# The scan of an RWKV-7 and Hyena block: ScalarE and VectorE in program order, the preparation in 35 pieces, weight splits one batch ahead

## The chip, the cores and the metric

The kernel runs on one core of a Trainium2 chip. The metric is device time in microseconds (us). A profiled execution gives the trace: the busy times of TensorE (PE, with PEld for its weight loads), VectorE (DVE), ScalarE (ACT) and GpSimd (POOL), the DMA queues (SyncE, SP, issues most of them), and the clock that TensorE was granted.

## The reference

Two layers on 256 latent tokens and 256 context tokens of width 2048. Layer 0 mixes tokens with RWKV-7: a recurrence over time in both directions, first over the context and then, from its final state, over the latents. Layer 1 mixes with Hyena (gated long convolutions by FFT). Each is followed by a squared-ReLU MLP, and everything is modulated by vectors computed from `c` (adaLN). The part that the change touches is the recurrence:

```python
def step(S, inp):
    w_t, k_t, v_t, kk_t, b_t = inp[:5]
    S = (S * w_t[:, :, None, :]
         - jnp.einsum('bhvk,bhk->bhv', S, kk_t)[..., None] * b_t[:, :, None, :]
         + v_t[..., None] * k_t[:, :, None, :])
    out = jnp.einsum('bhvk,bhk->bhv', S, inp[5]) if emit else None
    return S, out
```

`S` is 64 x 64 for each of 32 heads; `v = xv @ w_v` and the readout's `r = xr @ w_r` are projections of the mixed tokens.

## The kernel before

The scan is done in chunks of 64 tokens, so that it becomes matrix products. Four heads make a group (`g`, 0 to 7); a group has 8 steps (`i`), four over the context and four over the latents, and each step handles one chunk forward and one backward. `rwkv_scan` (line 780) loops over groups and steps, and cuts each step into three slots (`j` = 0, 1, 2; `n = 3 * i + j` counts the 24 slots of a group).

The chain that runs from step to step is `scan_step` (line 1086), one piece a slot. Slot 0: PE multiplies the chunk's values `VU` and the state `Z` into `pr`, ACT copies it to `rhs` (line 1112). Slot 1: PE applies the inverted triangular matrix `Y`, and ACT writes the result into `VU` (lines 1130 and 1131). Slot 2: PE makes the new state, ACT copies it to `Z` (line 1142). On PE other work stands between these:

- `scan_products` (line 985): the next step's matrices, masked and copied out of PSUM to `NT` by DVE and `KR` by ACT and DVE. Its diagonal matrices (line 993) come from DVE.
- `scan_prepare` (line 1020): the whole preparation of group g + 1, a generator that is advanced by `SCHED[n]` pieces a slot. `scan_prep` makes the operands of four units (two streams, two pairs of heads) from loads of `kx`, `rb`, `cum`, `a` and, for the latents, `rx`. `scan_m` makes the matrices `Mn` to invert. Then 31 rounds of two DVE instructions each (lines 1047 and 1049) invert 32 x 32 blocks; two DVE transposes (lines 1054 and 1055) and ACT's copies with masks (lines 1059 and 1060) write them into `Y`; the products `G` and `py` join the blocks.
- `scan_readout`: norm, bonus and gate of group g - 1, one piece a step at slot 2.
- `ada_scan`: adaLN products, one unit a step.
- `fill_v` and `fill_r` (lines 729 and 747): the projections `v` of group g + 1 and `r` of group g + 2, six pieces a step in slots 1 and 2. Their weights are loaded by SP (`fr`, line 712) and split into two parts by ACT (`fh`, line 133) and DVE (`flo`, line 134); their tokens `fx` are loaded by POOL.

In the last group the Hyena filters take the place of the fills.

What sets the order: a planner simulates the program at compile time and orders each engine's instructions and each DMA queue by priority and simulated readiness. Within the scan PE alone is bound to the program's order: `product` (line 71) ties each product to the one before it by an edge that is only used in planning (`pinned`). The pieces of the chain run at priority `PRI`, the next step's products at `PRJ`. ACT, DVE, SP and POOL are ordered by the planner. At run time each engine executes its instructions in the order it was given. Three PSUM buffers `sg` serve products, preparation and readout in turn.

The functions of the kernel that the change touches, with the line numbers of the profile:

Of the kernel before, what the change touches and what calls it, by code (L numbers as in the profile page):

```python
# [18 lines left out]
P = 128  # L19
# [22 lines left out]

class Kern:
    def __init__(self, nc, tc, I, out, scr, upto=99):
        self.nc, self.tc, self.I, self.out, self.scr = nc, tc, I, out, scr
        self.bg, self.credit, self.rate = [], 0.0, 0.0
        self.upto = upto
        self.wraw, self.wsp = [], []
# [21 lines left out]

    def product(self, out, lhsT, rhs, **kw):

        r = self.nc.tensor.matmul(out, lhsT=lhsT, rhs=rhs, **kw)  # L73
        if self.pinned:
            if self.pinned is not True:
                self.tc.add_manual_dep(r.ins, self.pinned.name, mybir.DependencyInfo(mybir.DependencyClass.NoSync, mybir.DependencyReason.DATA),
                                       reason="order of the scan")
            self.pinned = r.ins
        return r

    pinned = None
# [646 lines left out]

    def fill_v(self, g):

        nc = self.nc
        ps = [self.fl.tile([P, 2, 256], F32, name="fl") for _ in range(2)]
        for k in range(KT):
            if k % 2 == 0:
                w = self.fill_w(self.I["w_v"][0], k, g)
            x = self.fill_x(self.scr["xv"][k])
            for tt in range(4):
                s = slice(tt * P, (tt + 1) * P)
                self.fill_mm(ps[tt // 2][:, tt % 2], (x[:, 0, s], x[:, 1, s]), [a[:, k % 2] for a in w], k, tt % 2)
                if tt % 2:  # L740
                    yield
        for j in range(2):
            t = self.fw.tile([P, 2, 256], F32, name="fe", bufs=2)
            nc.scalar.copy(t, ps[j])
            nc.sync.dma_start(self.scr["v"][g, j * 256 : (j + 1) * 256, :].rearrange("(a p) n -> p a n", p=P), t)

    def fill_r(self, g):
        nc = self.nc
        ps = self.fl.tile([P, 2, 256], F32, name="fl")
        for k in range(0, KT, 2):  # L750
            w = self.fill_w(self.I["w_r"][0], k, g)
            x = self.fill_x(self.scr["xr"][k // 2])
            for q in range(2):
                for i in range(2):
                    self.fill_mm(ps[:, i], [a[:, q, i * P : (i + 1) * P] for a in w],
                                 [x[:, j, q * L : q * L + L] for j in range(2)], k + q, i)
                yield
        t = self.fw.tile([P, 2, 256], F32, name="fe", bufs=2)
        nc.scalar.copy(t, ps)
        nc.sync.dma_start(self.scr["r"][g * 256 : (g + 1) * 256, :].rearrange("(a p) n -> p a n", p=P), t)  # L760

# [7 lines left out]
    def rwkv_begin(self):  # L769

        self.bg = [self.urgent(self.scan_prepare(0), self.PRB)]
        n = 80 - self.NLOW
        for _ in self.beside(self.fill_r(0), 16, itertools.islice(self.low, n // 8), n // 8 + .1):
            self.tick(6.0 / (16 + n // 8))
        for _ in self.beside(itertools.chain(self.fill_v(0), self.fill_r(1)), 48, self.low, n - n // 8 + .1):
            self.tick(self.BEG)
        self.drain()


    def rwkv_scan(self, es, prep_pools, ngroups=KT // 2):  # L780
# [17 lines left out]
        self.pinned = True  # L798
        for g in range(ngroups):

            last = g + 1 == ngroups
            prep = iter(()) if last else self.scan_prepare(g + 1)
            read = self.scan_readout(g - 1) if g else iter(())
            take = lambda it, n: [None for _ in itertools.islice(it, n)]
            if not last:
                fill = itertools.chain(self.fill_v(g + 1), self.fill_r(g + 2) if g + 2 < ngroups else ())
            else:
                prep_pools.close()
# [3 lines left out]
            for i in range(8):  # L812
                nxt = self.scan_products(g, i + 1) if i < 7 else () if last else self.scan_products(g + 1, 0)
                step = self.scan_step(g, i)
                for j in range(3):
                    with self.tc.high_priority(self.PRI):
                        next(step)
                    if j == 0:
                        with self.tc.high_priority(self.PRJ):
                            for _ in nxt:  # L820
                                pass
                    take(prep, self.SCHED[3 * i + j])
                    if j == 1:
                        take(ada, 1)
                    if j == 2:
                        take(read, 1)
                    if last:
                        pin, self.pinned = self.pinned, None
                        with self.tc.issue_after(pin):
                            take(fill, self.NFILT)  # L830
                        self.pinned = pin
                    elif j:
                        take(fill, 3)
                if i == 5 and last:
                    pin, self.pinned = self.pinned, None
                    take(late, 1)
                    self.pinned = pin
            take(prep, 99), take(read, 99), take(fill, 99)
            self.grp.pop(g - 1, None)
        self.pinned = None  # L840
# [3 lines left out]


    SCHED = (2, 1, 2, 1, 2, 1, 0, 2, 2, 1, 2, 2, 2, 2, 2, 2, 2, 2, 1, 1, 1, 0, 2, 2)
# [4 lines left out]
    def scan_open(self, es, prep_pools):  # L851

        self.loaded, self.unit = [], 0
# [46 lines left out]

    def scan_prep(self, g, pi, st, eend, res):
# [7 lines left out]
        if st == 1:  # L909
            rx = ld.tile([P, L], F32, name="rx")  # L910
            nc.sync.dma_start(rx, scr["r"][m * P : (m + 1) * P, :])
        yield
# [3 lines left out]
        eexc = ex[:, 0:524].rearrange("p (d x) -> p d x", d=2)[:, :, 0:260].rearrange("p d (c t) -> p d c t", t=65)[:, :, :, 0:64]  # L916
        nc.scalar.activation(einc, c4(cum), AF.Exp, scale=-EH)
        nc.scalar.copy(eend[:, st, pi, 0, :], ex[:, 64:260:65])
        nc.scalar.copy(eend[:, st, pi, 1, :], ex[:, 261:521:65])
        ei = tp.tile([P, 2, L], F32, name="ei")  # L920
        nc.scalar.activation(ei, cum, AF.Exp, scale=EH)
        bc = lambda a: a[:].unsqueeze(1).broadcast_to([P, 2, L])
        bc4 = lambda a: a[:].rearrange("p (c t) -> p c t", t=64).unsqueeze(1).broadcast_to([P, 2, 4, 64])
        nc.vector.scalar_tensor_tensor(kk, kx, self.col("k_k", m), kk, op0=ALU.mult, op1=ALU.mult)

        KB = self.kbp[g % 2].tile([P, 2, 2, 4, 64], F32, name="KB", bufs=4)
        nc.vector.tensor_tensor(KB[:, 1], c4(a), c4(ei), op=ALU.mult)
        nc.vector.tensor_tensor(KB[:, 1], KB[:, 1], bc4(kk), op=ALU.mult)

        nc.vector.tensor_tensor(self.ard_view(g, pi, 4 * st), bc4(kk), eexc, op=ALU.mult)  # L930
        res["KB", pi, st] = KB
        yield

        kd = KB[:, 0]
        nc.scalar.activation(kd, c4(a), AF.Identity, scale=self.hka[:, 0, m : m + 1], bias=self.hka[:, 1, m : m + 1])
        nc.vector.tensor_tensor(kd, kd, bc4(kx), op=ALU.mult)
        if st == 1:
            nc.vector.tensor_tensor(self.ard_view(g, pi, 3), bc4(rx), einc, op=ALU.mult)
# [3 lines left out]
            nc.vector.tensor_tensor(q4, kd[:, 0], kd[:, 1], op=ALU.add)  # L942
            nc.vector.scalar_tensor_tensor(q, rx, self.col("r_k", m), q, op0=ALU.mult, op1=ALU.mult)
            res["q", pi] = q
        nc.vector.tensor_tensor(kd, kd, c4(ei), op=ALU.mult)
# [39 lines left out]
    def scan_products(self, g, i):  # L985
# [4 lines left out]
        if il == 0:  # L990
            for pi in range(2):
                D_ = self.ard_view(g, pi, 1 + st).rearrange("p d c t -> p (d c) t")
                nc.vector.tensor_tensor(D_, self.id2[:].unsqueeze(1).broadcast_to([P, 8, 64]),
                                        eend[:, st, pi].rearrange("p d c -> p (d c)").unsqueeze(2).broadcast_to([P, 8, 64]), op=ALU.mult)
# [25 lines left out]
    def scan_prepare(self, g):  # L1020
# [21 lines left out]
        nc.gpsimd.memset(fl(W)[:, 0:1024:33], 1.0)  # L1042
        tmp = gp.tile([P, 256], F32, name="tmp", bufs=1)
# [10 lines left out]
        nc.vector.transpose(V[1][:].rearrange("p b t -> p t b"), W[:])  # L1054
        nc.vector.transpose(V[0][:].rearrange("p b t -> p t b"), W[:].rearrange("p i j -> p j i"))

        for d in range(2):
            src = V[d][:, 16 * d : 16 * d + 16, :]
            nc.scalar.activation(Y[:, d, :, 0:32], src, AF.Identity, scale=self.masks[:, 0, 1, 31:32])
            nc.scalar.activation(Y[:, d, :, 32:64], src, AF.Identity, scale=self.masks[:, 1, 0, 31:32])  # L1060
# [4 lines left out]
        for d in range(2):  # L1065
# [5 lines left out]
            for h in range(2):  # L1071
                (nc.vector.tensor_copy if h else nc.scalar.copy)(G[part(h, 1), 16 * d : 16 * d + 16, :], ph[part(h, 1)])
            yield
        py = self.sg.tile([P, 16, 32], F32, name="sg")
        for d in range(2):
# [5 lines left out]
            yield  # L1081
        for d in range(2):
            for h in range(2):
                (nc.scalar.copy if h else nc.vector.tensor_copy)(Y[part(h, d), d, :, 32 - 32 * d : 64 - 32 * d], py[part(h, d)])

    def scan_step(self, g, i):
# [10 lines left out]
        VU = cp.tile([P, 2, 2, 2, 64], F32, name="VU", bufs=3)  # L1097
        for d in range(2):
            c = il if d == 0 else 3 - il
            t0 = st * L + 64 * c  # L1100
            src = scr["v"][g, t0 : t0 + 64, :].rearrange("s (p h v) -> h s p v", h=2, v=64)
            for h, hp in enumerate(hs):
                nc.sync.dma_start(VU[hp, :, d, h, :], src[h])
# [537 lines left out]
```

## Time and profile before

| | us |
|---|---|
| three runs | 3831.64, 3811.79, 3830.21 (median 3830.21) |
| profiled execution | 3833.14 |
| its span, first to last instruction | 3831.4 |
| PE busy | 3414.8 (89%) |
| DVE busy | 2495.3 (65%) |
| ACT busy | 1749.9 (46%) |
| POOL busy | 685.3 (18%) |
| mean granted TensorE clock | 0.938 |

Busy shares are means over the span; the stages differ, so the prediction reads them by window. In rows of waits, "A <- B: total, times, longest" says that the instructions A of an engine stood until B released them.

### The profile page before, as it was taken

To read this page: it belongs to the slowest core of one execution; us is meant where nothing else is said; L and a number is where in the kernel's file an instruction comes from. 1 tells how busy PE (TensorE), PEld (TensorE's weight loads), DVE (VectorE), ACT (ScalarE), POOL (GpSimd) and SP (SyncE) were. 2 spreads that over 40 slices of the span, in tenths; PEclk is the share of its full clock that TensorE was granted. 3 is DMA by queue.
4 is the path that set the end of the run, shared out by engine and by line. 5 is a ranking of instruction groups with operands and counts; after the bars stand their busy time and mean duration, and the time that the engine had idled before them with its cause. 6 is when DMAs were issued, how large, how long until landed. Compare 5 with 4: busy or idle time off the path is not lost. (4 is left out here: it accounts for less than half of the span.)

```text
span 3831.4 us, 82336 instructions
## 1 busy us (share of the span) xinstructions
PE 3414.8 (89%) x34206; PEld 3134.3 (82%) x34206; DVE 2495.3 (65%) x3841; ACT 1749.9 (46%) x3061; POOL 685.3 (18%) x706
## 2 busy tenths in 40 slices
PE   7799887887788778899999999989999899999997
PEld 3377676776777675789999999989888799999997
DVE  5887676546654555568776777587787675556554
ACT  4444444433434344444343434465565663435352
POOL 2622220101111000020000000523443830000002
PEclk9899898888888888999999999999999899999998
DMA  9577797876777664558888887666665776556553
GB/s 323 188 235 258 250 318 226 236 214 209 219 222 220 206 172 129 173 180 288 278 264 276 269 275 238 205 194 207 215 217 174 229 231 185 180 186 187 183 182 110
DMA packets 694367, 838.34 MB, mean 219 GB/s; under 512 B 81055, under 2 KB 562240, under 8 KB 693992
## 3 DMA queue, kind: packets, MB, share of 16 engines
q1 hardware_dynamic: 662888, 719.82, 59.8%
q0 software_dynamic: 31104, 113.26, 9.6%
q8 instruction: 268, 4.39, 0.5%
q14 instruction: 107, 0.88, 0.1%
HBM read 778.36 MB, written 54.59 MB: 217 GB/s over the span
## 5 line engine op out<-in xcount | busy, mean ns | idle before, releaser
L134 DVE TENSOR_TENSOR wl<-w,wh 128x1024 fp32r<-128x1024 f32 (+1 forms) x716 | 924.1, 1295 | 564.8 <-ACT wh L133 559.7
L133 ACT CAST wh<-w 128x1024 fp32r<-128x1024 f32 (+1 forms) x716 | 740.4, 1043 | 770.5 <-PE mm L128 473.2
L127 PE MATMUL mm<-hxh,wh 128*128 128x258 f32 (+1 forms) x3072 | 871.5, 285 | 22.6 <-ACT hxh L398 18.1
L129 PE MATMUL mm<-hxh,wl 128*128 128x258 f32 (+1 forms) x3072 | 872.0, 285 | 9.0 <-DVE wl L134 8.8
L128 PE MATMUL mm<-hxl,wh 128*128 128x258 f32 (+1 forms) x3072 | 874.2, 285 | 0.5 <-DVE hxl L399 0.5
L127 PEld LDWEIGHTS mm<-hxh,wh 128*128 128x128 f32 x3072 | 582.3, 190 | 26.3 <-ACT hxh L398 19.0
L129 PEld LDWEIGHTS mm<-hxh,wl 128*128 128x128 f32 x3072 | 582.1, 190 | 13.8 <-DVE wl L134 11.9
L128 PEld LDWEIGHTS mm<-hxl,wh 128*128 128x128 f32 x3072 | 584.8, 190 | 3.7 <-DVE hxl L399 1.8
L128 PE MATMUL mm<-ul,wh 128*128 128x256 f32 x2048 | 579.3, 283 | 9.5 <-DVE ul L134 9.5
L127 PE MATMUL mm<-uh,wh 128*128 128x256 f32 x2048 | 578.5, 283 | 5.8 <-ACT uh L133 5.5
L129 PE MATMUL mm<-uh,wl 128*128 128x256 f32 x2048 | 578.2, 283 | 0.1
L262 POOL TENSOR_TENSOR acc<-acc,aw 128x512 f32<-128x512 f32 x180 | 274.0, 1523 | 909.9 <-ACT aw L260 876.5
L128 PEld LDWEIGHTS mm<-ul,wh 128*128 128x128 f32 x2048 | 391.3, 191 | 10.4 <-DVE ul L134 10.4
L127 PEld LDWEIGHTS mm<-uh,wh 128*128 128x128 f32 x2048 | 391.0, 191 | 6.4 <-ACT uh L133 5.9
L129 PEld LDWEIGHTS mm<-uh,wl 128*128 128x128 f32 x2048 | 391.8, 191 | 0.5 <-DVE wl L134 0.5
L266 DVE SCALAR_TENSOR_TENSOR acc<-aw,sc,acc 128x512 f32<-128x512 f32 x300 | 231.9, 773 | 103.1 <-DMA aw<-in_ada_w 100.5
L73 PE MATMUL fl<-fh,fx 128*128 128x256 f32 x1024 | 224.6, 308 | 8.4 <-DMA fx<-xv 5.1
L73 PEld LDWEIGHTS fl<-fh,fx 128*128 128x128 f32 x1024 | 177.8, 205 | 32.7 <-issue 21.5
L73 PE MATMUL sg<-ard,KB 64*64 64x64 f32 (+1 forms) x3584 | 145.6, 260 | 49.3 <-DVE dv L1193 22.9
L260 ACT ACTIVATE aw<-aw,sc 128x512 f32<-128x512 f32 x180 | 126.1, 719 | 125.4 <-DMA aw<-in_ada_w 122.0
L73 PEld LDWEIGHTS sg<-ard,KB 64*64 64x64 f32 x3584 | 124.2, 148 | 60.6 <-DVE dv L1193 24.2
L720 POOL DMA_DIRECT2D fx<-xv x128 | 67.8, 529 | 574.2 <-PE fl L73 552.8
(376 smaller groups left out, 6209.6 us busy)
## 6 DMA issues: line engine op xcount, KB each, us to landing
aw<-in_ada_w SPq DMA_DIRECT2D x288, 512.0 KB, 5.1
w<-in_mlp_down SPq DMA_DIRECT2D x128, 1024.0 KB, 5.4
w<-in_mlp_up SPq DMA_DIRECT2D x120, 1024.0 KB, 6.1
fx<-xv POOLq DMA_DIRECT2D x128, 512.0 KB, 5.3
aw<-in_ada_w SPq DMA_DIRECT2D x192, 256.0 KB, 3.8
w<-in_hy_in_w SPq DMA_DIRECT2D x44, 1024.0 KB, 5.3
fx<-xr POOLq DMA_DIRECT2D x64, 512.0 KB, 5.3
w<-in_w_k SPq DMA_DIRECT2D x16, 1024.0 KB, 7.7
```

Source lines behind the costliest of these rows:

```text
L73: r = self.nc.tensor.matmul(out, lhsT=lhsT, rhs=rhs, **kw)
L127: nc.tensor.matmul(out, lhsT=wh, rhs=xh, start=first, stop=False)
L128: nc.tensor.matmul(out, lhsT=wh, rhs=xl, start=False, stop=False)
L129: nc.tensor.matmul(out, lhsT=wl, rhs=xh, start=False, stop=last)
L133: self.nc.scalar.copy(hi, f32)
L134: (eng or self.nc.vector).tensor_tensor(lo, f32, hi, op=ALU.subtract)
L260: nc.scalar.activation(w[:, a] if k + a else acc, w[:, a], AF.Identity, scale=s)
L262: nc.gpsimd.tensor_tensor(acc, acc, w[:, a], op=ALU.add)
L266: nc.vector.scalar_tensor_tensor(acc, w[:, a], s, acc, op0=ALU.mult, op1=ALU.add)
L720: self.nc.gpsimd.dma_start(x, src)
```

## The change

- The order of ACT and DVE in the scan is bound as PE's is. `Nc` and `Ordered` wrap the two engines, and every instruction that the scan traces on them is tied to the one before it (`pin`); the last group's filters are left out of it. The products' priority `PRJ` becomes `PRI`.
- The preparation is cut anew: `yield`s move, the two transposes are two pieces, the `yf` activations follow the products of `G`, and the order of units and `scan_m` is written out in `scan_prepare`. 35 pieces are taken by the new `SCHED`; the 36th (the copies into `Y`) is taken at the start of the next group, ahead of its products.
- In `scan_prep`, ACT makes `ei`, `ex`, `eend` and `KB[:, 0]` in the first piece; `rx` is loaded ahead by `load_r`.
- The diagonals of the latents (`scan_diag`) are made at slots 6 and 7; readout pieces are taken at slots 6, 7, 9, 13, 14 and 16.
- The `VU` loads of a step (`scan_values`) are written one step ahead, at slot 1.
- The fills' weights go through a feed: `feed_load` issues the load, `feed_hi` the ACT part, `feed_lo` the DVE part and the next load, at fixed places in the slots; a fill takes a split that is ready. The copies of a fill's results (`fe`) move into its last pieces.
- Both copies of `G` are made by DVE (one was ACT's). Ahead of the scan, the preparation of group 0 is advanced by 4 pieces beside `fill_r(0)`, where it was 6.

```diff
+class Ordered:
+    def __getattr__(self, name):
+        f = getattr(self.engine, name)
+        def call(*a, **kw):
+            return self.kern.pin(self.key, f(*a, **kw))
+        return call
...
+    def pin(self, key, r):
+        if self.pins is not None:
+            prev = self.pins.get(key)
+            if prev is not None:
+                self.tc.add_manual_dep(r.ins, prev.name, mybir.DependencyInfo(mybir.DependencyClass.NoSync, mybir.DependencyReason.DATA),
+                                       reason="order of the scan")
+            self.pins[key] = r.ins
+        return r
...
+    def feed_load(self):
+        f, nxt = self.fed, next(self.feed, None)
+        if nxt:
+            W, k, g = nxt
+            raw = self.fw.tile([P, 2, 256], F32, name="fr")
+            self.nc.sync.dma_start(raw, W[k * P : (k + 2) * P, g * 256 : (g + 1) * 256].rearrange("(k p) n -> p k n", p=P))
+            f["ld"].append(raw)
+    def feed_hi(self):
+        f = self.fed
+        if f["ld"] and len(f["hi"]) + len(f["ok"]) + f["use"] < 2:
+            raw = f["ld"].pop(0)
+            hi = self.fw.tile([P, 2, 256], F32R, name="fh", bufs=2)
+            self.nc.scalar.copy(hi, raw)
+            f["hi"].append((raw, hi))
+    def feed_lo(self):
+        f = self.fed
+        while f["hi"]:
+            raw, hi = f["hi"].pop(0)
+            lo = self.fw.tile([P, 2, 256], F32R, name="flo", bufs=2)
+            self.nc.vector.tensor_tensor(lo, raw, hi, op=ALU.subtract)
+            f["ok"].append((hi, lo))
+            self.feed_load()
+    def feed_take(self, W, k, g):
+        f = self.fed
+        if self.feed is None:
+            return self.fill_w(W, k, g)
+        if not f["ok"]:
+            self.feed_hi()
+            self.feed_lo()
+        f["use"] = 1
+        return f["ok"].pop(0)
...
                 for j in range(3):
+                    n = 3 * i + j
                     with self.tc.high_priority(self.PRI):
+                        if not last:
+                            self.feed_lo()
                         next(step)
-                    if j == 0:
-                        with self.tc.high_priority(self.PRJ):
+                        if j == 0:
+                            take(prep, i == 0 and not last)
                             for _ in nxt:
                                 pass
-                    take(prep, self.SCHED[3 * i + j])
+                            if not last:
+                                self.feed_hi()
+                        if j == 1 and i < 7:
+                            self.scan_values(g, i + 1)
+                        elif j == 1 and not last:
+                            self.scan_values(g + 1, 0)
+                        take(diag, n in self.DIAG)
+                    take(prep, self.SCHED[n])
                     if j == 1:
                         take(ada, 1)
-                    if j == 2:
-                        take(read, 1)
+                    take(read, n in self.READ)
...
                     elif j:
                         take(fill, 3)
+                        self.feed_hi()
...
-    SCHED = (2, 1, 2, 1, 2, 1, 0, 2, 2, 1, 2, 2, 2, 2, 2, 2, 2, 2, 1, 1, 1, 0, 2, 2)
+    SCHED = (1, 1, 1, 2, 1, 2, 1, 1, 2, 1, 1, 2, 1, 2, 2, 1, 2, 2, 1, 2, 2, 1, 2, 1)
+    DIAG = (6, 7)
+    READ = (6, 7, 9, 13, 14, 16)
...
-        for st, pi in ((0, 0), (0, 1), (1, 0)):
-            yield from self.scan_prep(g, pi, st, eend, res)
-        yield from self.scan_m(g, 0, Mn, res)
+        U = {(st, pi): self.scan_prep(g, pi, st, eend, res) for st in range(2) for pi in range(2)}
+        M = [self.scan_m(g, st, Mn, res) for st in range(2)]
+        for _ in range(2):
+            yield next(U[0, 0])
+        yield next(U[0, 1])
+        next(U[0, 1])
+        yield from self.scan_diag(g, 0)
+        yield next(U[1, 0])
+        yield next(M[0])
+        yield next(U[1, 0])
+        yield next(M[0])
         self.scan_bonus(0, res)
-        yield from self.scan_prep(g, 1, 1, eend, res)
-        yield from self.scan_m(g, 1, Mn, res)
+        yield next(U[1, 1])
+        yield next(M[1])
+        yield next(U[1, 1])
+        yield next(M[1])
         self.scan_bonus(1, res)
...
         nc.vector.transpose(V[1][:].rearrange("p b t -> p t b"), W[:])
+        yield
         nc.vector.transpose(V[0][:].rearrange("p b t -> p t b"), W[:].rearrange("p i j -> p j i"))
-        for d in range(2):
-            src = V[d][:, 16 * d : 16 * d + 16, :]
-            nc.scalar.activation(Y[:, d, :, 0:32], src, AF.Identity, scale=self.masks[:, 0, 1, 31:32])
-            nc.scalar.activation(Y[:, d, :, 32:64], src, AF.Identity, scale=self.masks[:, 1, 0, 31:32])
         yield
...
-                (nc.vector.tensor_copy if h else nc.scalar.copy)(G[part(h, 1), 16 * d : 16 * d + 16, :], ph[part(h, 1)])
+                nc.vector.tensor_copy(G[part(h, 1), 16 * d : 16 * d + 16, :], ph[part(h, 1)])
+            src = V[d][:, 16 * d : 16 * d + 16, :]
+            nc.scalar.activation(Y[:, d, :, 0:32], src, AF.Identity, scale=self.masks[:, 0, 1, 31:32])
+            nc.scalar.activation(Y[:, d, :, 32:64], src, AF.Identity, scale=self.masks[:, 1, 0, 31:32])
             yield
```

More of the change, by code (lines that the diff above doesn't have):

```diff
@@ L68, in turn @@
         return pools[0]
-    def product(self, out, lhsT, rhs, **kw):
[L73 to L81, printed above, removed]
+    def pin(self, key, r):
[6 more added lines that the diff above has]
+        return r
+    def product(self, out, lhsT, rhs, **kw):
+        return self.pin("pe", self.nc.tensor.matmul(out, lhsT=lhsT, rhs=rhs, **kw))
+    pins = None
     def tick(self, n=1.0):
@@ L851, in scan_open @@
     def scan_open(self, es, prep_pools):
-        self.loaded, self.unit = [], 0
+        self.loaded, self.unit, self.rx = [], 0, []
         self.ard, self.yf, self.kbp = [None] * 2, [None] * 2, [None] * 2
@@ L1095, in scan_step @@
         N, KR = res["N", i], res["KR", i]
[L1097 to L1103, printed above, removed]
+        VU = res.pop(("VU", i))
         pr = self.sc.tile([P, 2, 4, 64], F32, name="sc")
```

131 lines of the change are left out of this document (93 added, 38 removed).

## The prediction

> **What bounds the kernel now.** I first split the span into stages with the view of engine busy time by window. The scan runs from 583.0 (its first `rhs` copy) to about 1570; 705.9 to 1328.9 are five whole groups of it, 1 to 5. Columns: stretch, length, then busy time of PE, PEld, DVE, ACT, POOL (with instruction counts), granted clock, DMA share, GB/s.
>
> ```profile
> core 0: us, PE busy (x) PEld busy (x) DVE busy (x) ACT busy (x) POOL busy (x), PEclk, DMA share, GB/s
> 583.00:705.90 122.90, 95.53 (x1876) 85.16 (x1872) 77.00 (x161) 53.89 (x127) 13.79 (x26) 0.85 0.76 225
> 705.90:1328.90 623.00, 495.08 (x9380) 442.01 (x9380) 348.29 (x755) 253.45 (x602) 68.93 (x130) 0.86 0.74 217
> 1328.90:1430.60 101.70, 81.62 (x1742) 73.08 (x1740) 49.81 (x116) 38.78 (x94) 7.98 (x15) 0.85 0.64 185
> 1430.60:1570.20 139.60, 118.65 (x1399) 85.60 (x1400) 70.98 (x136) 62.80 (x136) 0.00 (x0) 0.89 0.41 126
> 1570.20:3831.40 2261.20, 2136.26 (x17180) 2097.84 (x17179) 1527.40 (x2027) 1071.80 (x1635) 410.65 (x358) 0.97 0.68 215
> ```
>
> A group of 1 to 5 takes 623.0/5 = 124.6 us. PE is busy 99.0 of it and idle 25.6; DVE is busy 69.7, ACT 50.7. No engine is full: PE, whose order is fixed, stands still for others. The clock of 0.86 against 0.97 later says that standing still costs twice. The same view over the 26 stretches of half clock in these groups (first, last, sum):
>
> ```profile
> 718.00:721.40 3.40, 2.94 (x74) 2.95 (x78) 0.03 (x1) 1.60 (x6) 0.00 (x0) 0.50 0.77 235
> ...
> 1315.30:1322.10 6.80, 5.68 (x53) 4.81 (x53) 1.08 (x2) 1.57 (x3) 0.53 (x1) 0.50 0.25 80
> sum 171.10, PE 138.38 PEld 124.13 DVE 102.30 ACT 59.84 POOL 6.86; mean PE 5.32 PEld 4.77 DVE 3.93 ACT 2.30 POOL 0.26
> ```
>
> PE worked 138.4 us at half clock; half of that, 69.2 us or 13.8 a group, is what the low clock added. At full clock and never waiting a group's PE work is 99.0 - 13.8 = **85.2 us**. Next, who keeps PE waiting in the five groups (total, times, longest), and behind whom DVE and ACT stand:
>
> ```profile
> PE sc L73 <- ACT Z L1142: 46.1, 19, 6.4
> PE sg L73 <- DVE dv L1193: 22.9, 6, 6.8
> PE sg L73 <- DVE KR L1017: 18.6, 8, 2.7
> PE sg L73 <- issue: 13.3, 7, 3.6
> PE fl L73 <- ACT fe L744: 10.9, 2, 5.5
> ...
> DVE flo L134 <- ACT fh L133: 74.8, 50, 3.8
> DVE rb L924 <- DMA rb<-ri: 58.4, 17, 5.6
> DVE ard L938 <- DMA rx<-r: 33.6, 5, 7.8
> DVE q L942 <- PE sg L73: 29.2, 5, 6.1
> ...
> ACT ex L917 <- DVE ard L938: 39.8, 8, 8.5
> ACT yf L1059 <- DVE d L1054: 19.3, 5, 5.4
> ```
>
> The waits of DVE and ACT are the roots of PE's. One case shows how, on the timeline of ACT and then of PE:
>
> ```profile
> 912.77 0.72 ACT L1059 ACTIVATE yf<-d,masks 128x512 f32<-128x512 f32 x1 [4.17 <-DVE d L1054]
> ...
> 916.23 0.35 ACT L1142 COPY Z<-sc 128x256 f32<-128x256 f32 x1
> ...
> 916.63 1.12 PE L73 MATMUL sc<-KR,VU 128*64 128x64 f32 x16 [6.39 <-ACT Z L1142]
> ```
>
> `Z` was next in the recurrence, but the planner had put four `yf` activations ahead of it on ACT, and these waited for the transposes on DVE. So what bounds the scan is work of the next group standing at the head of ACT and DVE before its inputs are there.
>
> **The change part by part.** All of it acts in the scan; the other stages keep their instructions, so I price them at 0. Durations and landings (DMA rows: KB each, us to landing) for the parts:
>
> ```profile
> L134 DVE TENSOR_TENSOR flo<-fr,fh 128x512 fp32r<-128x512 f32 x81 | 55.8, 689 | 74.9 <-ACT fh L133 74.8
> L133 ACT CAST fh<-fr 128x512 fp32r<-128x512 f32 x80 | 49.2, 615 | 89.9 <-PE fl L73 56.6 <-issue 18.5 <-DMA fr<-in_w_r 14.7
> L917 ACT ACTIVATE ex<-cum 128x512 f32<-128x512 f32 x20 | 12.5, 627 | 41.3 <-DVE ard L938 39.8 <-issue 1.1 <-DVE mod L307 0.4
> L921 ACT ACTIVATE ei<-cum 128x512 f32<-128x512 f32 x20 | 12.6, 630 | 22.8 <-DVE KB L945 14.5 <-DMA cum<-cum 8.3
> L935 ACT ACTIVATE KB<-a,hka 128x512 f32<-128x512 f32 x20 | 16.2, 812 | 2.0 <-PE sg L73 1.5
> L1072 DVE COPY d<-sg 32x512 f32<-32x512 f32 x10 | 6.6, 693 | 6.5 <-ACT d L1072 6.4
> L1084 ACT COPY yf<-sg 32x512 f32<-32x512 f32 x10 | 5.8, 578 | 7.8 <-DVE yf L1084 7.6
> L1047 DVE TENSOR_TENSOR tmp<-d,d 128x31 f32<-128x31 f32 (+15 forms) x155 | 52.8, 341 | 5.0
> ...
> fr<-in_w_v SPq DMA_DIRECT2D x40, 256.0 KB, 4.7
> VU<-v SPq DMA_DIRECT2D x160, 32.0 KB, 3.6
> rb<-ri SPq DMA_DIRECT2D x38, 64.0 KB, 5.1
> rx<-r SPq DMA_DIRECT2D x10, 128.0 KB, 3.3
> ```
>
> (1) `yf` moves behind the transposes: the two transposes become two pieces, and the activations follow the products of `G`. The block of 5.5 us a group or more (the row above: 6.39) goes from the 46.1/5 = 9.2 that PE waits for `Z`. I take 5.5; bounds 3.9 (19.3/5, ACT's own wait) and 9.2. (2) `rx` is loaded two slots ahead. A slot is a third of a step, 124.6/24 = 5.2 us now, so it has about 10 us for a landing of 3.3. That ends DVE's 33.6 and ACT's 39.8 us of waiting. The parts of a unit are respaced, readout goes to slots 6, 7, 9, 13, 14, 16, and the product that frees `q` now precedes its next writer. Together they aim at the waits for `dv` (22.9/5 = 4.6 a group) and `KR` (18.6/5 = 3.7). I take 4.0 and 2.7; bounds 0, if the `rb` waits stay, and all 8.3. (3) The `fe` copies move into the last pieces of a fill: 10.9/5 = 2.2, taken whole. (4) The splits of the fills' weights run a batch ahead. PE hardly waited for them, so this is worth nothing directly. It matters because `flo` held DVE 74.8 us; in a fixed order that wait would have blocked everything behind. The cover is four fill pieces, more than one slot, against 0.615 + 0.689 us. If a weight (landing 4.7) is late, ACT stands at `fh` with `VU` and `Z` behind it. (5) `G` leaves ACT: DVE gets two copies of 0.69 a group, 1.4 us, beside PE work, since DVE has 124.6 - 69.7 = 55 us free. (6) The `VU` loads, four DMAs on SP a step, are asked for a step earlier in the program; the landing of 3.6 fits two slots. SP's and POOL's order stays the planner's. (7) The order itself adds no instruction, but it adds these new stalls. At slot 0 ACT has, ahead of `VU`, the two `Y` copies (2 x 0.58), `fh` (0.62) and the unit's `ei`, `ex`, `KB` (2.07): 3.85 us. PE covers about 2.2 by 18 fill products (18 x 2136.26/17180 us) and more by its other products, so the stall is 0 to 3.9; I take 1.5. In steps 4 and 5 DVE must fit 20 of 31 elimination rounds, two instructions each at the mean of 0.34, so 14 us or more, beside flo, masks and readout into some 22 us of PE work. It falls behind by 0 to 4; I take 2.0.
>
> **The sum.** Idle a group: 25.6 - (5.5 + 4.0 + 2.7 + 2.2) + 1.5 + 2.0 = 14.7. The wait on issue, 13.3/5 = 2.7, is in it; it stays. The half clock follows long waits, and the longest are those that go: I take a third of the 13.8, 4.6 (bounds 0 and 13.8). So 85.2 + 14.7 + 4.6 = **104.5 us a group**. Groups 0 to 5 take 122.9 + 623.0 = 745.9 now and 627 then: -119. Group 6 (101.7, idle 20.1) gains in proportion, 20.1 x 20.1/25.6: -16. Group 7 (139.6) is held by the filters: -2. Opening the feed before the loop, two loads and splits, lies beside the first products: 0 to 6, say +2. Together -135. The profiled execution took 3833.1 us (span 3831.4), 2.9 above the median of 3830.2, so I say **3695 us** for the median.
>
> A page weighs one term otherwise. The Trainium skill, TensorE: Matmul & The Clock Gate, section "Why this matters for your kernels", asks for no PE gap over some 3 us if the clock is to stay full. By it my 4.6 would be near 0, as nearly all such gaps go, and the time near 3665. The trace agrees only in part: waits of 1.29 and 1.70 us were enough for a half-clock stretch.
>
> ```profile
> 811.83 0.51 PE L73 MATMUL sc<-rhs,yf 64*64 64x64 f32 x10 [1.29 <-ACT rhs L1112]
> ...
> 815.89 0.98 PE L73 MATMUL sg<-d,Mn 32*32 32x32 f32 x50 [1.70 <-issue]
> ...
> 817.00:820.40 3.40, 3.40 (x20) 2.70 (x13) 1.79 (x3) 0.85 (x2) 0.00 (x0) 0.50 0.41 126
> ```
>
> **The rivals.** *Better than forecast.* All waits but issue go. Then DMA is next: its share of 0.74 of 124.6 is 92.2 us of transfer a group, and a share of 0.95 makes 97: 745.9 - 582 = 164, and 20 on group 6, about 3646. Against it: the steps 4 and 5 above.
>
> *The queues give half back.* DMA's share would be 0.88 at 104.5 us, and the scan has never shown more than 0.76 over a group. If loads land late and hold the share at 0.82, a group takes 92.2/0.82 = 112.4: -71, and -16 for group 6: 3743. For it: SP blocks behind loads whose buffer isn't free (first row of the next fence). Against: 500 to 600 us moved 296 GB/s at 0.93.
>
> ```profile
> SPq L296 <- PE mm L73: 67.9, 23, 8.2
> ...
> 500.00:600.00 100.00, 80.59 (x1005) 71.54 (x1004) 65.34 (x132) 46.88 (x100) 16.80 (x31) 0.89 0.93 296
> ```
>
> *Slower: a fixed order passes every late operand on to PE.* DVE's `rb` multiply opens each unit, its loads still stand in SP's planned order, and everything behind it on DVE (NT, KR, flo) waits too; the planner had at least spread these. DVE's waits for DMA at `rb` and `rx`, 92.0/5 = 18.4 a group, with ACT's at `fh` and `cum`, (14.7 + 8.3)/5 = 4.6, would reach PE whole: 23. Each us of PE idle has brought 13.8/25.6 = 0.54 us of half clock, so with issue and a few short waits (6): 85.2 + 29 x 1.54 = 130, or +5.4 a group, about 3862 for six groups. It decides from (124.6 - 85.2)/1.54 = 25.6 us of waiting. Against: those loads have three slots or more in the new spacing. The Trainium skill states in the same page, section "Architectural detail", that ScalarE and VectorE are strict first in, first out; the trace's `Z` behind `yf` agrees.
>
> *It doesn't do what it says.* The planner's old order was mostly the program's, so the new edges bind little, and gains and new stalls cancel: 3830.
>
> **How the numbers follow.** Forecast 0.50, better 0.08, queues 0.17, slower 0.16, no effect 0.09. The range 3640 to 3840 holds the first three and the last, about 0.82; the forecast's own range, groups of 98 to 111, is 3651 to 3739. A change under 0.5% (19 us, the spread of the three runs) can't be told from none. Faster is 0.50 + 0.08 + 0.17 = 0.75, same 0.09, slower 0.16.
>
> **What would show it.** Right: a group of 100 to 109 us, PE's clock over 0.92 in the scan, no wait for `Z` over 3 us, no `rx` wait on DVE, DMA share near 0.88, the longest steps 4 and 5. Wrong: `rb`, `fr` or `VU` DMA at the head of PE's, DVE's or ACT's waits (late loads); a group over 115 us; or stages outside the scan that differ by more than 10 us.

## The result, and the profile after

The changed kernel takes 3771.06 us (median of four runs, 3767.86 to 3779.49) beside 3830.62 for the kernel before on the same chip: a ratio of 0.9859, interval 0.9825 to 0.9894. The ratio is one of means: by the medians the gain is about 60 us, by the ratio about 54, where 135 were forecast. The sign held, and the time lies in the range of 3640 to 3840 us, though outside the forecast's own 3651 to 3739; the size is less than half.

The profiled execution took 3769.96 us, its span 3768.1 against 3831.4. The view of engine busy time by window, cut at the same places as before: group 0, groups 1 to 5, group 6, group 7, the rest. Columns as in the prediction.

```profile
582.20:683.90 101.70, 89.54 (x1836) 79.28 (x1831) 66.07 (x145) 44.96 (x110) 13.78 (x26) 0.92 0.83 249
683.90:1268.50 584.60, 488.39 (x9385) 431.61 (x9380) 357.72 (x765) 247.41 (x591) 68.92 (x130) 0.88 0.81 233
1268.50:1372.20 103.70, 84.41 (x1780) 73.66 (x1780) 70.40 (x150) 48.27 (x114) 7.99 (x15) 0.86 0.69 201
1372.20:1503.80 131.60, 116.05 (x1390) 84.57 (x1392) 70.05 (x134) 61.08 (x133) 0.00 (x0) 0.90 0.41 128
1503.80:3768.10 2264.30, 2139.78 (x17196) 2102.75 (x17192) 1529.19 (x2028) 1073.57 (x1636) 408.98 (x358) 0.97 0.68 215
```

| stage | before | forecast change | measured change |
|---|---|---|---|
| ahead of the scan | 583.0 | +2 | -0.8 |
| group 0 | 122.9 | -18 | -21.2 |
| groups 1 to 5 | 623.0 | -100.5 | -38.4 |
| group 6 | 101.7 | -16 | +2.0 |
| group 7 | 139.6 | -2 | -8.0 |
| after the scan | 2261.2 | 0 | +3.1 |

Group 0 came out about as forecast. It differs from groups 1 to 5 in two parts of the work: there is no readout of a group before it, and the copies into `Y`, which the other groups make at their start, were made ahead of the scan. The shortfall is 62 us in groups 1 to 5, 12.4 a group (116.9 against 104.5), and 18 in group 6. Groups 1 to 5 can be split as in the prediction with the sum over their 23 stretches of half clock:

```profile
sum 137.17, PE 119.61 PEld 102.94 DVE 72.28 ACT 45.42 POOL 5.85; mean PE 5.20 PEld 4.48 DVE 3.14 ACT 1.97 POOL 0.25
```

Idle (584.6 - 488.39)/5 = 19.2 a group (before 25.6, forecast 14.7); half-clock extra 119.61/2/5 = 12.0 (before 13.8, forecast 4.6); work at full speed 97.7 - 12.0 = 85.7 (85.2). So of the 12.4 us that are missing 4.5 are idle time, 7.4 half clock and 0.5 work. Who keeps PE waiting now, and two of the waits of DVE and ACT, in the same window (total, times, longest):

```profile
PE sg L110 <- DMA sqo<-v: 29.8, 14, 6.4
PE sg L110 <- ACT yf L53: 18.1, 5, 3.8
PE sc L110 <- ACT Z L53: 13.9, 15, 2.3
PE fl L110 <- DMA fx<-xv: 10.1, 7, 2.6
PE sg L110 <- issue: 8.1, 4, 2.9
...
PE sg L110 <- ACT KR L53: 1.8, 5, 0.4
...
DVE bs L53 <- PE sg L110: 29.6, 9, 8.2
...
ACT VU L53 <- PE sc L110: 21.7, 5, 6.9
```

L110 is now the helper of every product and L53 the wrapper of every ACT and DVE instruction, so groups are told apart by tile. The waits for `Z`, `KR`, `dv` and `fe` that led PE's list are gone or small. Two new ones are at its head: a DMA, `sqo<-v`, and the `Y` copies (`yf`). The first is a step of the readout: it loads the values `v` to make the bonus. The timeline around one of them, SP, DVE, PE and ACT in order of time:

```profile
839.22 0.48 DVE L53 SCALAR_TENSOR_TENSOR dv<-dv,cols,sqo 128x256 f32<-128x256 f32 x1 [0.48 <-ACT sqo L53]
839.87 2.91 SPq L970 DMA_DIRECT2D VU<-v  x4
842.88 1.50 SPq L1315 DMA_DIRECT2D sqo<-v  x2
...
850.07 1.08 PE L110 MATMUL sg<-ident,sqo 64*64 64x64 f32 x11 [3.37 <-DMA sqo<-v]
...
851.50 0.42 DVE L53 TENSOR_TENSOR bs<-sg,bs 128x256 f32<-128x256 f32 x1 [5.34 <-PE sg L110]
852.18 0.78 ACT L53 ACTIVATE VU<-sc 64x256 f32<-64x256 f32 x2 [4.04 <-PE sc L110]
```

The values go into buffer `sqo`, where the readout's deviation stood. So the load can't start before DVE's multiply of `dv` has read it (839.2, slot 7). Then it stands on SP behind the four `VU` loads that the change put into the same slot (2.91 us). It lands some 7 us after its issue, and the product that reads it is due in slot 9. PE stands for 3.37 us, and DVE and ACT with it, since their orders are fixed behind what PE makes. The second pair of heads does the same from slot 14 to 16. The DMA rows (KB each, us to landing) of the kernel before, and then of the changed one, show that the landings of these loads also became longer (`VU` took 3.6 before):

```profile
fx<-xv POOLq DMA_DIRECT2D x80, 512.0 KB, 4.9
...
sqo<-v SPq DMA_DIRECT2D x20, 64.0 KB, 6.0
```

```profile
fx<-xv POOLq DMA_DIRECT2D x80, 512.0 KB, 6.5
...
VU<-v SPq DMA_DIRECT2D x160, 32.0 KB, 5.1
...
sqo<-v SPq DMA_DIRECT2D x20, 64.0 KB, 6.5
```

The other new wait is at the start of a group. The copies of the finished `Y` alternate between DVE and ACT (four in turn, each waiting for the one before; first and last shown), and hold the PSUM buffer that the next step's products need:

```profile
917.97 0.67 DVE L53 COPY yf<-sg 32x512 f32<-32x512 f32 x1
...
920.06 0.58 ACT L53 COPY yf<-sg 32x512 f32<-32x512 f32 x1 [0.75 <-DVE yf L53]
...
920.69 1.44 PE L110 MATMUL sg<-ard,KB 64*64 64x64 f32 x34 [3.77 <-ACT yf L53]
```

Theory after this: the late values load costs most of what is missing. Rivals: the queues are full (the prediction's second rival; the DMA share of 0.81 is near its 0.82); or the bound order itself passes on whatever is late, load or not.

### The profile page after: what moved, and what is told of

Same layout as the page of the kernel before. It is cut to its first block, busy times and chain, and to the rows that moved or that the text cites. A ratio compares the mean times of both kernels' runs of the same rounds, so it can differ in the third digit from the quotient of the medians.

```text
span 3768.1 us, 82300 instructions
## 1 busy us (share of the span) xinstructions
PE 3402.8 (90%) x34206; PEld 3119.8 (83%) x34206; DVE 2513.1 (67%) x3857; ACT 1741.7 (46%) x3045; POOL 684.7 (18%) x706
## 4 chain that ended last, share of the span: by engine, by line
PE 43%; DMA 15%; DVE 10%; issue 9%; ACT 4%; POOL 3%; SPq 1%; POOLq 0%; ACTq 0%; DVEq 0%
PE mm L158 11%; PE mm L159 11%; PE mm L160 11%; DMA aw<-in_ada_w 7%; PE fl L110 3%; DMA w<-in_mlp_up 2%; DVE wl L53 2%; PE sg L110 2%; PE sc L110 2%; POOL acc L293 2%; DMA sqo<-v 2%; DVE acc L53 1%; DMA fx<-xv 1%; ACT wh L53 1%; ACT aw L53 1%
## 5 line engine op out<-in xcount | busy, mean ns | idle before, releaser
L53 DVE TENSOR_TENSOR wl<-w,wh 128x1024 fp32r<-128x1024 f32 (+1 forms) x716 | 925.4, 1296 | 552.9 <-ACT wh L53 542.4
L53 ACT CAST wh<-w 128x1024 fp32r<-128x1024 f32 (+1 forms) x716 | 741.4, 1044 | 775.7 <-PE mm L159 479.3
L158 PE MATMUL mm<-hxh,wh 128*128 128x258 f32 (+1 forms) x3072 | 873.2, 286 | 23.3 <-ACT hxh L53 18.1
L53 DVE SCALAR_TENSOR_TENSOR acc<-aw,sc,acc 128x512 f32<-128x512 f32 x300 | 230.9, 770 | 105.9 <-DMA aw<-in_ada_w 103.3
L110 PE MATMUL fl<-fh,fx 128*128 128x256 f32 x1024 | 233.7, 315 | 21.7 <-DMA fx<-xv 19.9
L110 PEld LDWEIGHTS fl<-fh,fx 128*128 128x128 f32 x1024 | 184.9, 212 | 43.2 <-DMA fx<-xv 24.9
L53 ACT ACTIVATE aw<-aw,sc 128x512 f32<-128x512 f32 x180 | 126.1, 719 | 134.3 <-DMA aw<-in_ada_w 126.8
L53 DVE TENSOR_TENSOR flo<-fr,fh 128x512 fp32r<-128x512 f32 x128 | 87.7, 686 | 124.8 <-ACT fh L53 120.5
L110 PE MATMUL sg<-ard,KB 64*64 64x64 f32 (+1 forms) x3584 | 135.0, 249 | 32.9 <-ACT yf L53 26.0
```

The lines of the kernel that those rows point to most:

```text
L53: return self.kern.pin(self.key, f(*a, **kw))
L110: return self.pin("pe", self.nc.tensor.matmul(out, lhsT=lhsT, rhs=rhs, **kw))
L158: nc.tensor.matmul(out, lhsT=wh, rhs=xh, start=first, stop=False)
```

## The experiments

Ratios are to the kernel before on the same chip; step times are means of groups 1 to 5. The changed kernel was also run again beside the last two experiments.

> The changed kernel as it is, on the same chip as the two kernels above, as their measure: ratio 0.983 to 0.989 to the kernel before.

It took 3777.85 us, ratio 0.9871 (0.9844 to 0.9898), and stands with 0.9859 as the base of what follows.

**The load left out.** The values load of groups 0 to 6 isn't issued; the product reads the buffer's old content, so the bonus part of the output is not computed from `v`.

```diff
-                V = rp.tile([P, L], F32, name="sqo", bufs=n)[:]...
-                for h in range(2):
+                V = (rp.tile([P, L], F32, name="sqo", bufs=n) if last else sq)[:]...
+                for h in range(2 if last else 0):
                     nc.sync.dma_start(V[64 * h : 64 * h + 64], src[h][:, :, pi, :])
```

> The changed kernel without the readout's load of the values in groups 0 to 6 (PE multiplies what stands in that buffer; the bonus is left wrong, the rest is unchanged). The price of that load under the bound order. Theory A: it is over half of what the forecast missed in groups 1 to 5: a group goes from 116.9 to 105 to 108, the time to 3700 to 3725 (ratio about 0.97). Theory B (another late load takes its place): above 3750.

3711.39 us, ratio 0.9692 (0.9670 to 0.9714): 0.0167 to 0.0179 below the changed kernel, 64 to 69 us. Groups 1 to 5 by window, their half-clock sum, and PE's waits:

```profile
680.40:1211.20 530.80, 464.36 (x9380) 410.47 (x9380) 357.64 (x765) 247.27 (x591) 68.91 (x130) 0.93 0.86 254
```

```profile
sum 71.70, PE 66.55 PEld 56.97 DVE 38.33 ACT 28.66 POOL 3.50; mean PE 5.55 PEld 4.75 DVE 3.19 ACT 2.39 POOL 0.29
```

```profile
PE sg L110 <- ACT yf L53: 18.9, 5, 3.8
PE sc L110 <- ACT Z L53: 13.5, 15, 1.7
PE sg L110 <- issue: 11.2, 6, 3.0
```

A group takes 106.2 us: idle 13.3, half-clock extra 6.7, work 86.2. So the load costs 10.8 us a group, 5.9 as idle time and 5.3 as half clock (work is 0.5 longer). Its traffic isn't the reason: 20 loads of 64 KB are 1.28 MB, 5.5 us over five groups at 233 GB/s if nothing else moved. The DMA share rose to 0.86 while the groups became shorter, so 0.81 was no ceiling: the queue rival falls as the cause.

**The readers of the load one slot later.** The load is kept, and so is its place; only the product that reads it moves from slots 9 and 16 to 10 and 17.

```diff
-    READ = (6, 7, 9, 13, 14, 16)
+    READ = (6, 7, 10, 13, 14, 17)
```

> The changed kernel with the readout's third pieces one slot later (slots 10 and 17 for 9 and 16), so three slots after the values load and not two. Theory A: the wait for the values falls from 31.8 us in five groups to under 8, time 3725 to 3745. Theory B: the load is late by its place in SP's queue and lands later too, the wait stays above 20, time within 10 us of 3771.

3728.02 us, ratio 0.9742 (0.9709 to 0.9775). PE's wait for the load, and groups 1 to 5:

```profile
PE sg L110 <- DMA sqo<-v: 16.8, 5, 4.8
```

```profile
680.40:1228.20 547.80, 469.53 (x9380) 414.69 (x9380) 356.43 (x765) 247.11 (x591) 68.92 (x130) 0.93 0.86 249
```

Two numbers bring 45 to 49 us. The wait fell less than was expected (16.8 us, not under 8). Of the 14 waits five are left, those of the first pair; step 5, which holds the second, goes from 17.4 to 11.2 us. A group takes 109.6, in the longest of the four executions (3741.99 us).

**The load made early instead.** Values are loaded in a pair's first piece into the gate's buffer, the gate into `sqo` after the `dv` multiply, and it is used a piece later.

```diff
-    READ = (6, 7, 9, 13, 14, 16)
+    READ = (6, 7, 9, 13, 14, 16, 18)
...
+            gt, V = (gate_load(), None) if last else (None, value_load())
...
-                yield from values()
+                gt = gate_load()
+                yield from values(V)
             nc.vector.scalar_tensor_tensor(dv, dv, self.col("lnx_b", m), bs, op0=ALU.add, op1=ALU.add)
+            if not last:
+                yield
             nc.vector.tensor_tensor(dv, dv, gt, op=ALU.mult)
             nc.sync.dma_start(scr["y"][m * P : (m + 1) * P, :], dv)
-            yield
+            if last:
+                yield
```

> The changed kernel with the readout's two loads exchanged: the values take the buffer of the gate and are loaded in a pair's first piece, the gate takes the buffer that frees later and is used a piece later; one more readout slot (18). Theory A (the missing gain is the readout: its values load waits for its buffer, then 6.5 us to land, and PE in its fixed order stands for it 31.8 us in groups 1 to 5, with half clock behind): that wait vanishes, a group of 1 to 5 goes from 116.9 to 107 to 110 us, the time from 3771 to about 3720 to 3735. Theory B (DMA as such is late, share 0.81 now): the wait moves to other loads (fx, fr, VU), a group stays above 114, the time above 3755.

3759.99 us, ratio 0.9820 (0.9791 to 0.9850), not told apart from the changed kernel by the intervals; a group takes 114.2 us. The wait for the load is gone, and another has come in its place, PE's first and its root on DVE:

```profile
PE sc L110 <- ACT Z L53: 35.6, 15, 6.2
...
DVE dv L53 <- DMA y<-dv: 18.6, 5, 4.7
```

The last use of `dv` moved to where the next pair begins, and that pair writes the same buffer: DVE waits for the store of `y`, ACT for DVE (42.8 us at the square, 22.1 in the changed kernel), PE for `Z`. The load's price was real, but this way of removing it builds the same stall with a store.

**The `Y` copies in the group before.** They move from the start of a group into slot 23.

```diff
-    SCHED = (1, 1, 1, 2, ..., 2, 1, 2, 1)
+    SCHED = (1, 1, 1, 2, ..., 2, 1, 2, 2)
...
-                            take(prep, i == 0 and not last)
```

> The changed kernel with the copies into Y taken in slot 23, right after their products, not at the start of the next group. Theory A: PE's wait of 3.7 us a group for the copies (18.6 us in groups 1 to 5) goes, with some half clock behind it: 3 to 6 us a group over seven groups, 3771 to about 3730 to 3750. Theory B (ACT and DVE then stand for the products in slot 23 and the wait only moves to slot 23 or to the next rhs): within 10 us of 3771.

3762.96 us, ratio 0.9836 (0.9808 to 0.9864): no difference that can be told from the changed kernel. Step 0 goes from 15.3 to 8.7 us, and step 1 gives most of it back (from 12.8 to 17.7). In the waits of PE, DVE and SP:

```profile
PE sg L110 <- ACT KR L53: 20.2, 5, 6.5
...
DVE rb L53 <- DMA rb<-ri: 30.2, 4, 9.0
...
SPq L1031 <- DMA r<-fe: 17.4, 5, 4.0
```

SP stands 3.5 us a group at the load of `rx`, which must follow the store of `r` that the fill has just made. The unit loads of `rb` stand behind it on SP. The changed kernel has the same stand (20.7 us in five groups); that the stall at the `Y` copies covers it there is argued, not measured.

**The later readers, the `Y` copies in slot 23, and `rx` behind the unit's loads.** The two edits together, and the `rx` load bound behind the loads of its unit on SP.

```diff
-            self.load_r(2 * g + (u + 1) % 2)
...
+            with self.tc.issue_after(self.last_load):
+                self.load_r(2 * g + (u + 1) % 2)
```

> The changed kernel with three edits: readout's third pieces a slot later (as in the run with slots 10 and 17), the copies into Y in slot 23, and the loads of rx ordered on SP behind the unit loads, as SP stood 4 us a group at rx, which waits for the store of r, with cum, a and rb of the next units behind it (then ACT and DVE waited for these, up to 9 us, in the run with Y copies in slot 23). If that is the root, the Y edit now pays: 3690 to 3715. If not, as the slots 10 and 17 alone or worse: 3725 to 3750.

3726.00 us, ratio 0.9729 (0.9698 to 0.9761), the same as the later readers alone. A group takes 107.8 us. PE's wait for the values falls to 8.0 us, but now `rx` itself is late: DVE waits for it at `ard`, 25.2 us in eight waits. The wait has been handed from one late transfer to the next.

**The layout without the order.** Only PE stays bound.

```diff
-        if self.pins is not None:
+        if self.pins is not None and key == "pe":
```

> The changed kernel, layout and feed as changed, but ACT and DVE not bound: only PE keeps the order of the program. Theory A (the bound order is what removes the blocks of yf before Z and of operand waits on DVE): the blocks come back, group 0 goes from 101.7 back to 115 or more, time 3800 to 3835. Theory C (the new layout of the pieces did it, the order on ACT and DVE adds little or costs): time at or below 3771.

3836.75 us, ratio 1.0031 (1.0016 to 1.0047).

```profile
705.20:1327.60 622.40, 490.81 (x9397) 433.74 (x9393) 356.45 (x765) 247.02 (x591) 68.91 (x130) 0.88 0.74 217
```

```profile
PE sg L110 <- DVE KR L53: 46.5, 10, 7.6
PE sc L110 <- ACT Z L53: 30.7, 19, 7.8
...
DVE rb L53 <- DMA rb<-ri: 53.5, 19, 5.5
```

124.5 us a group and 123.9 for group 0: the new pieces, slots and feed are worth nothing while the planner orders ACT and DVE. It again lets DVE wait at `rb` with `KR` behind. The values load stands at the same slots here, and PE waits for it 5.3 us in the five groups.

**The order without the layout.** The kernel before, with ACT and DVE bound to its program's order.

```diff
+        nc = Nc(self, nc)
...
-        self.pinned = True
+        self.pins = {}
```

> The kernel before with one part of the change: ACT and DVE bound to the program's order, its old layout, SCHED, readout and splits kept. Theory A (bound order pays only with a layout made for it): the yf activations stand ahead of Z by the program now, the splits' wait for fh blocks DVE, rx is loaded just ahead of its use; 3840 to 3950 us, slower than before. Theory C (order alone is the gain): 3760 to 3800.

4022.47 us, ratio 1.0510 (1.0481 to 1.0539), 151 us a group, slower still than expected. PE's waits in its groups 1 to 5:

```profile
PE fl L108 <- ACT fh L52: 105.3, 54, 6.5
PE fl L108 <- DVE flo L52: 91.9, 51, 5.4
PE sc L108 <- ACT Z L52: 7.1, 15, 0.5
```

The chain is served (`Z` 7.1 us), and the fills stand for their splits: 39 us a group.

**The order and the layout without the feed.** The feed isn't opened, and a fill makes its split when it needs it.

```diff
-        self.feed_open(ngroups)
+        self.fed = {"ld": [], "hi": [], "ok": [], "use": 0}
```

> The changed kernel with the feed undone: each fill loads and splits its weights where it uses them, under the bound order. Theory A (in a fixed order the cast waits for the fill's own buffers and everything behind it waits too): each of 16 splits a group costs about 1 to 2 us, 3790 to 3880. Theory D (the feed is worth nothing, as PE hardly waited for splits before): within 10 us of 3771 (ratio 0.983 to 0.988).

3964.63 us, ratio 1.0351 (1.0326 to 1.0376), 143.4 us a group, again more than expected:

```profile
PE fl L110 <- ACT fh L53: 91.6, 50, 4.2
PE fl L110 <- DVE flo L53: 61.4, 50, 3.3
```

Under a bound order the splits one batch ahead are worth 0.048 to 0.049 of the time, some 185 us. In this layout the order pays only with them.

**Two versions that put it together.** One has the late readers (slots 10 and 17), `Y` in slot 23 and `rx` loaded one unit earlier behind that unit's loads. The other, in place of the late readers, has the early values load, but with the pair's last use of `dv` in a piece of its own and eight readout slots (6, 7, 9, 11, 13, 14, 16, 18).

```diff
-        if g and 0 < u % 4 < 3:
-            self.load_r(2 * g + (u + 1) % 2)
         if g:
             self.load_to(u + self.AHEAD)
+        if g and u % 4 < 2:
+            with self.tc.issue_after(self.last_load):
+                self.load_r(2 * g + u % 4)
```

> As the run with slots 10 and 17, Y in slot 23 and rx behind the unit loads, but rx loaded one unit earlier. Theory A: the waits of DVE for rx (25 us in five groups there) go, 3700 to 3715 us (ratio 0.965 to 0.970). Theory B: 3720 to 3735, no gain from it.

> The changed kernel with the readout's values loaded in a pair's first piece into the gate's buffer, the gate loaded later and used in a fourth piece (slots 6, 7, 9, 11 and 13, 14, 16, 18), the copies into Y in slot 23, and rx loaded one unit earlier and behind that unit's loads on SP. Theory A (the three late inputs were what kept PE waiting): groups 1 to 5 at 102 to 106 us, 3685 to 3710 us, faster than all runs so far (ratio 0.962 to 0.968). Theory B (DMA share is 0.86 to 0.9 by now, another load comes late): 3715 to 3740, about as the run with slots 10 and 17.

3716.94 us, ratio 0.9709 (0.9676 to 0.9742), and 3715.65 us, ratio 0.9710 (0.9670 to 0.9751). Both are some 1.6% below the changed kernel (0.9871) and faster than both kernels; between the two no difference can be told. Both miss the lower of their two expected ranges by 2 to 6 us, though the group of the second, 104.4, lies in its 102 to 106. The one with the early load, by window, half-clock sum and PE's waits in groups 1 to 5:

```profile
684.10:1205.90 521.80, 460.82 (x9384) 405.97 (x9380) 357.64 (x765) 246.55 (x592) 68.92 (x130) 0.95 0.89 262
```

```profile
sum 51.20, PE 46.76 PEld 40.32 DVE 29.68 ACT 15.98 POOL 3.10; mean PE 5.84 PEld 5.04 DVE 3.71 ACT 2.00 POOL 0.39
```

```profile
PE sc L110 <- ACT rhs L53: 14.1, 7, 6.3
PE sc L110 <- ACT Z L53: 13.8, 15, 2.9
PE sg L110 <- issue: 9.2, 5, 3.1
```

104.4 us a group: idle 12.2, half-clock extra 4.7, work 87.5, at a DMA share of 0.89. The load is issued, and no wait for it is among PE's. That is the length of group that was forecast for the changed kernel, but by another sum: 2.5 less idle time and 2.3 more work, and that the two cancel is luck. In the other version a group takes 107.9, and the load is still first among PE's waits:

```profile
PE sg L110 <- DMA sqo<-v: 24.8, 7, 5.1
```

So the late reader doesn't end the wait, and what each edit of these two versions is worth can't be told apart.

## Why the prediction was right in sign and wrong in size

**The step that failed** is the readout's move in part (2): "readout goes to slots 6, 7, 9, 13, 14, 16 ... Together they aim at the waits for `dv` ... and `KR`". The move was costed only by the waits that it takes away; the DMA that a readout piece issues, the values load, was put at nothing, without a reason. Both waits did go (DVE's `KR`, 18.6 us, and `dv`, 22.9, are out of PE's list), 8 us a group. But slots 7 to 9 leave two slots to free a buffer, pass four `VU` loads on SP and land in 6.5 us. With the load left out the group is 10.8 us shorter, of the 12.4 that were missing. Reading it a slot later gets 7.3 of that back. Loading it early brought 2.7 while the store of `y` stood in its place, and 12.5 together with three further edits. The row of the kernel before for this load, 6.0 us to landing, stood in the view that was read for the other loads; two slots of the forecast group are 2 x 104.5/24 = 8.7 us, and behind the four `VU` loads (2.9 us here) that leaves 5.8, less than the landing.

**What held.** The `yf` block: PE's wait for `Z` fell from 9.2 to 13.9/5 = 2.8 us a group, 6.4 against 5.5, none over 2.3. The `rx` wait on DVE and the `fe` wait are gone. Group 0, with all of the change but the readout and the `Y` copies, gave 21.2 where 18.4 were forecast. The feed was rightly called worth nothing directly and needed under a fixed order; its size, 185 us, had not been worked out. No stage outside the scan moved by more than 3.1 us. Group 7 gave 8.0 where 2 were forecast: some 4 of it is a stall that now falls into group 6 (below), the rest is open. Of the prediction's own signs of being wrong, a group over 115 us came true; the DMA at the head of PE's waits was none of the three that it named.

**New stalls.** "At slot 0 ACT has, ahead of `VU`, the two `Y` copies": the place was right, the way was not. The `Y` copies alternate between two engines and hold a PSUM buffer; PE waits 18.1/5 = 3.6 us a group where 1.5 were taken. "In steps 4 and 5 DVE must fit 20 of 31 elimination rounds": no lag came of it in groups 1 to 5. Step 4 takes 12.4 us, and step 5, 17.4 us, takes 12.3 with the load left out. Together 3.5 were taken; with the load out, idle was 13.3 against 14.7.

**The half clock.** "The half clock follows long waits ...: I take a third of the 13.8" is the second term that failed: 4.6 was taken, 12.0 measured. The load accounts for 5.3 of the 7.4 between them. With the load out, at less idle time than forecast, it is still 6.7; the ratio that the prediction's own slower rival used, 0.54 us a us of idle, would have given 14.7 x 0.54 = 7.9.

**Group 6** was given a share in proportion, -16, and moved by +2.0: 18 us of the shortfall. PE's idle time there stayed (20.1 and 19.3 us), though its wait for `Z` fell from 12.7 to 2.0. By step, steps 4 to 6 gained 12.2 us, but steps 0 to 3 take 7.8 longer, and step 7 takes 21.1 where it took 14.7. The load explains 4.7 (99.0 us with it left out). The version with the early load takes 92.2, 11.5 less: 5.0 of it in step 3, which held the wait for the load, and 6.5 in step 0, which held the `Y` copies. In step 7 PE stands for DVE:

```profile
1354.98 0.68 PE L110 MATMUL sc<-ard,Z 64*64 64x64 f32 x16 [2.69 <-DVE tmp L53]
```

`tmp` is the elimination, so here a lag of DVE did come: it is busy for 15.8 of the 21.1 us, before for 4.8 of 14.7. In the whole group it has 70.40 us of work where it had 49.81, since the planner no longer moves preparation into earlier groups. The step also ends with a stall of 4.2 us at the `Y` copies for group 7, which the last group takes ahead of its first step; in the kernel before this stall, also 4.2, lay inside group 7. DVE's lag isn't shown to be the whole cause: with DVE unbound (52.6 us of work there) group 6 took 106.6. The rest stays open.

**The rivals.** *The queues give half back* comes nearest in time (112.4 a group, 3743) and in share (0.82 assumed, 0.81 measured), but not in cause: shares of 0.86 and 0.89 came with shorter groups. *Slower: a fixed order passes every late operand on to PE* is a real mechanism: it made the old layout 5.1% slower, though by the fills' splits and not by the `rb` and `rx` loads that it priced, and the values load is its largest case in the changed kernel. *It doesn't do what it says* is refuted by the pair of runs: the layout alone +0.3%, the order alone +5.1%, both -1.4%.

## What to carry to other kernels

When a step is moved, list what it issues, not only what it computes: for each DMA, when its buffer comes free, which transfers are queued ahead of it, its landing time from the profile, and how many slots later it is read. Here binding the engines' order paid only together with a layout in which the operands are early; the layout alone was worth nothing, and the order alone cost 5%. Under the bound order two of the stalls that were removed (by the early load, by the `Y` copies in slot 23) uncovered the next late transfer, and brought no gain that can be told.

## What the runs showed of the hardware

**Standing still cost about one and a half times its length.** As an average over groups 1 to 5, half-clock extra for each us of PE idle: 0.54 before, 12.0/19.2 = 0.63 after, 6.7/13.3 = 0.50 with the load out, 4.7/12.2 = 0.39 in the version with the early load. The Trainium skill, TensorE: Matmul & The Clock Gate, section "Why this matters for your kernels", asks for no gap over some 3 us; the trace agrees in part. In the version with the early load all three gaps over 3 us (6.33, 3.12 and 3.10) came with a stretch of half clock, and so did all 16 in these groups of the kernel before and all 10 in the changed one. But a wait of 2.85 us was followed by none, and one of 1.76 us by a stretch of 6.8 us. PE's timeline and the window:

```profile
739.58 0.69 PE L110 MATMUL sc<-KR,VU 128*64 128x64 f32 x16 [2.85 <-ACT Z L53]
...
879.66 0.51 PE L110 MATMUL sc<-rhs,yf 64*64 64x64 f32 x10 [1.76 <-ACT rhs L53]
```

```profile
881.84:888.66 6.82, 5.71 (x82) 4.70 (x76) 3.86 (x6) 3.14 (x6) 0.00 (x0) 0.50 0.43 134
```

So the length of a gap alone doesn't decide; what else does is not shown. All eight stretches in that window last 3.4, 6.8 or 10.2 us.

**A landing read from the kernel before doesn't hold for a changed one.** From the kernel before to the changed one the DMA share went from 0.74 to 0.81, the 512 KB loads of `fx` from 4.9 to 6.5 us and the 32 KB loads of `VU` from 3.6 to 5.1. But the share alone doesn't make it: the layout without the order has the old share of 0.74, and its `VU` loads took longer too (`fx` 5.3):

```profile
VU<-v SPq DMA_DIRECT2D x160, 32.0 KB, 4.6
```

With the values load left out, at 0.86, `VU` took 4.5; and from the kernel before to the changed one `rx` became shorter, 3.3 to 2.2 us. What sets the landing of each load is not shown.
